# Recurrent branch projections as pairs of wide and narrow matmuls, with the opening and the attention heads reordered

## The chip, the core and the metric

The kernel runs on one core of one Trainium2 chip. The core has a matrix engine (TensorE, PE in the profile, with its weight loads as PEld), VectorE (DVE), ScalarE (ACT), GpSimd (POOL) and a queue engine (SyncE, SP) that issues transfers. The engines run their own instruction queues in order and wait for each other by semaphores. Matmuls write PSUM, a memory of eight banks; everything else lives in SBUF. The metric is the device time of one execution in microseconds; lower is better.

## The reference

Two residual layers on 256 tokens of 2048 features in float32. Layer 0 mixes tokens with attention (16 query heads, 4 key and value heads, RMS norm of queries and keys, axial rotary positions), layer 1 with a gated recurrence. Each is followed by a SwiGLU feed-forward layer of width 5632.

```python
def recurrent_mixer(h, w_in, conv_w, conv_b, w_a, b_a, w_i, b_i, lam, w_out):
    xy = h @ w_in
    xb, yb = jnp.split(xy, 2, axis=-1)
    yb = jax.nn.gelu(yb, approximate=True)
    xb = depthwise_conv_centred(xb, conv_w, conv_b)
    h_fwd = rg_lru(xb, w_a[0], b_a[0], w_i[0], b_i[0], lam[0], reverse=False)
    h_bwd = rg_lru(xb, w_a[1], b_a[1], w_i[1], b_i[1], lam[1], reverse=True)
    out = (h_fwd + h_bwd).astype(h.dtype) * yb
    return out @ w_out

def reference(x, ...):
    for i in range(DEPTH):
        h = rms_norm(x, norm_mix[i])
        mix = attention_mixer(...) if i % N_MIXERS == 0 else recurrent_mixer(...)
        x = x + mix
        x = x + swiglu(rms_norm(x, norm_ffn[i]), ffn_w_gate[i], ffn_w_up[i], ffn_w_down[i])
    return x
```

## The kernel before

Activations lie with features on the partitions and the 256 tokens along the row, in 16 tiles of 128 features. To keep float32 accuracy every operand is split in two parts that the matrix engine takes at its fast rate: hi (rounded) and lo (the rest). A product needs three of the four partial products: hi·hi, hi·lo and lo·hi.

**Weights.** `half()` (L124) takes the next block from a list `order` (L114 on): 8 tiles of 128 x 128, 512 KB. `load_half` (L84) issues its transfer into `raw` on SP, casts it to `hi` on ACT (L93), and writes the difference `lo` on DVE (L94). raw, hi and lo have five buffers each, so loads run ahead of PE by at most five blocks.

**Two forms of projection.** `project` (L168) uses `blocks` (L159): for each weight tile one matmul of 512 columns (the hi weights against the activation's hi and lo side by side) and one of 256 columns (the lo weights against hi) that adds into the right half of the PSUM bank, so that the result is the sum of the bank's two halves. `project_sum` (L179) uses `three` (L174): three matmuls of 256 columns into one half of the bank; nothing is left to be summed, and the other half is free as work space. Attention and feed-forward layers use pairs; the recurrent branch projections and the last down projection use threes.

**PE's order is written by hand.** `step()` (L145) is called after every weight tile and counts a clock; `later(d, f)` puts a piece of work (scores, transposes, gate matmuls) into PE's stream d steps on. The constants KEYS, VALUE, USUAL, LATE, WHEN and WHEN_LAST (L39 to L45) are such delays. The order on ACT, DVE, POOL and SP is planned by the framework from a model of costs.

**Opening.** The key projection runs first: eight blocks, each of 4 feature tiles for 2 of the 4 key heads (L363). The input x arrives in 256 KB or 512 KB pieces between them (`load_x`, L318), is scaled by the norm's gains on ACT (L252), and its lo part is made on DVE (L255). The 1/rms of the first norm is applied late; its squares are taken from a second copy of x in token order, four loads of 512 KB into `raw` buffers (`token_squares`, L332). Then come four value projections and 16 query heads (`attend`, L420): rotary on POOL (L374 to L376), split on DVE (L213, L214), squares (L437), scores (L442), softmax, scaling on POOL (L457), transposes (`turn`, L463), product with the values (L472).

**Output projections** (`output`, L188) of both mixers work through the first halves of four outputs, then through 6 of the 8 tiles of the second halves of two, and only then need the mixer's last two tiles.

**Recurrent stage** (L657 on): eight blocks of 256 channels. In each iteration PE runs two convolution branch projections of the next block, two gelu branch projections of this one, and between them this block's gate matmuls. `conv_branch` (L558) multiplies the projection by 1/rms (`nr.r`) from PSUM into an SBUF row with borders (L563), takes the first tap on ACT into the bank's free half (L565), three more on DVE (L568), and splits the result (L213, L214) for the gates. `gelu_branch` (L574) multiplies by 1/rms into the bank's free half, which holds the branch until the block is finished.

Of the kernel before, what the change touches and what calls it, by code (L numbers as in the profile page):

```python
# [18 lines left out]
P = 128  # L19
S = 256  # L20
# [36 lines left out]
AXES = [64 * a + 32 * h + f for h in range(2) for a in range(2) for f in range(32)]  # L57


@with_exitstack  # L60
def trunk(ctx, tc, w, out):
# [22 lines left out]
    def load_half(src, n, pieces=None):  # L84
# [3 lines left out]
        for a, b, then in pieces or ((0, n, None),):  # L88
            sl = slice(a, b)
            sync.dma_start(out=raw[:, sl, :], in_=src[:, sl, :])  # L90
            if then:
                then()
            act.copy(hi[:, sl, :], raw[:, sl, :])  # L93
            dve.tensor_tensor(lo[:, sl, :], raw[:, sl, :], hi[:, sl, :].bitcast(F32), ALU.subtract)  # L94
        return [(hi[:, i, :], lo[:, i, :]) for i in range(n)]
# [9 lines left out]
    def ffn_order(l):  # L105
# [3 lines left out]
        for p, n in enumerate(PARTS):  # L109
            more = units[at[p + 1] : at[p + 2]] if p + 1 < len(PARTS) else []  # L110
            seq += more[:1] + [halves(w[f"w_down{l}_{p}"][j], n) for j in range(KT)] + more[1:]
        return sum(seq, [])

    order = [(w["w_k"][i], HALF) for i in range(2 * KT // 4)]  # L114
# [9 lines left out]
    def half():  # L124
        n = taken[0]
        taken[0] += 1
        if n == 0:
            x2 = [partial(load_x, 2 * i, 2) for i in range(2)]
            return load_half(*order[n], ((0, 2, x2[0]), (2, 4, x2[1]), (4, HALF, None)))
        if n < KT // 2 and n % 2 == 0:  # L130
            load_x(2 * n, 4)
        if n == KT // 2 - 2:
            load_tables()
        if KT // 2 - 1 <= n < KT // 2 + 3:
            token_squares(n - KT // 2 + 1)
# [32 lines left out]
    def project(xs):  # L168
        acc = new_acc()
        for k0 in range(0, len(xs), HALF):  # L170
            blocks(acc, half(), xs, k0, len(xs))
# [7 lines left out]
    def project_sum(xs):  # L179
# [6 lines left out]
        return acc, bank[:, S:]  # L186

    def output(xs, ready, norm, close):  # L188
# [3 lines left out]
        late = [half() for j in range(2)]  # L192
# [4 lines left out]
        for j in range(KT):  # L197
            if j < 2:
# [5 lines left out]
        norm.finish_later()  # L204

    def evac(acc, tag):
        t = tmp(tag, bufs=3 if tag == "hy" else 2)
        act.copy(t, acc[:, S:])  # L208
# [3 lines left out]
    def split(dst, src):  # L212
        dve.tensor_copy(dst[:, :S], src)  # L213
        dve.tensor_tensor(dst[:, S:], src, dst[:, :S].bitcast(F32), ALU.subtract)  # L214

# [22 lines left out]
    class Norm:  # L238
# [9 lines left out]
        def scale(self, k, eng=act):  # L248
            g = col(self.g[0], self.g[1] + k)
            t = xp.tile([P, 2 * S], F32R, tag="xg", name=nm("xg"), bufs=16)  # L250
            if eng is act:
                act.activation(t[:, :S], x_sb[k], AF.Copy, scale=g)  # L252
            else:
                eng.tensor_scalar(t[:, :S], x_sb[k], g, 1.0, ALU.mult, ALU.mult)
            dve.scalar_tensor_tensor(t[:, S:], x_sb[k], g, t[:, :S].bitcast(F32), ALU.mult, ALU.subtract)  # L255
            self.xs.append(t)

# [9 lines left out]
        def finish_later(self):  # L267
            later(NORM, self.finish)
# [30 lines left out]
    def table_op(i):  # L299
        if prev[0] is not None:  # L300
            tc.add_manual_dep(
                i.ins, prev[0].ins.name,
                mybir.DependencyInfo(mybir.DependencyClass.NoSync, mybir.DependencyReason.DATA),
                reason="activation tables",
            )
# [12 lines left out]
    def load_x(k0, n):  # L318
        a = k0 % 4
        sync.dma_start(out=xq[k0 // 4][:, a : a + n, :], in_=w["x"][:, k0 : k0 + n, :])  # L320
        for k in range(k0, k0 + n):
            n0.scale(k)
# [9 lines left out]
    def token_squares(c):  # L332
        raw = wp.tile([P, HALF, P], F32, tag="raw", name=nm("raw"), bufs=5)
        sync.dma_start(out=raw, in_=w["xt"][c])
        act.activation(raw, raw, AF.Square, accum_out=msq[:, c // 2, c % 2 : c % 2 + 1])
# [11 lines left out]
    def first_rms():  # L347
# [3 lines left out]
        dg = tmp("hq")  # L351
# [3 lines left out]
        r_t.append(rsqrt(ms, "rt0"))  # L355
        pst = ps_m.tile([P, 2 * S], F32, tag="pm", name=nm("pm"))
# [6 lines left out]
    for i in range(2 * KT // 4):  # L363
        wt = half()
        for j in range(2):
            blocks(k_acc[2 * (i % 2) + j], wt[4 * j : 4 * j + 4], n0.xs, 4 * (i // 2))
# [11 lines left out]
    def key(h, acc):  # L378
        y = evac(acc, "hy")
        sq = tmp("hsq")  # L380
# [16 lines left out]
    kT = [ap.tile([P, 2 * S], F32R, tag=f"kT{h}", name=f"kT{h}", bufs=1) for h in range(NKV)]  # L397
    vt = [ap.tile([P, 2, 2, P], F32R, tag=f"vt{h}", name=f"vt{h}", bufs=1) for h in range(NKV)]
    for h in range(NKV):
        key(h, k_acc[h])  # L400
# [15 lines left out]
    for h in range(NKV):  # L416
        value(h, project(n0.xs))
    sync.dma_start(out=pk[:, PK0:], in_=w["pk"][:, PK0:])

    def attend(h, acc, dst):  # L420
        late = h >= NQ - 1
        eng = dve if late else pool
        d_sum, d_sc, d_turn, d_val = LATE[h - NQ] if h >= NQ - 2 else USUAL
# [5 lines left out]
        split(qs, q)  # L429
# [9 lines left out]
        def scores():  # L439
# [8 lines left out]
            dve.tensor_tensor(mx, mx, f, ALU.mult)  # L448
# [29 lines left out]

        later(d_sum, sums)
# [40 lines left out]
    def ffn(l, norm, nxt):  # L520
# [13 lines left out]
        for p, n in enumerate(PARTS):  # L534
            last = p == len(PARTS) - 1
            cur = hid
            hid = [] if last else [unit(bounds[p + 1])]
            for j in range(KT):
                if last and j == KT - 1:
                    dve.tensor_tensor(x_sb[j], x_sb[j], project_sum(cur)[0], ALU.add)  # L540
                    if nxt is not None:
                        nxt.add(j)
                else:
                    add_residual(j, project(cur), nxt if last else None)
# [12 lines left out]
    scope.append(rt.enter_context(tc.tile_pool(name="rp", bufs=2)))  # L557
    def conv_branch(ct):  # L558
        acc, run = project_sum(nr.xs)
# [3 lines left out]
        dve.tensor_tensor(b[:, 2 : S + 2], acc, nr.r, ALU.mult)  # L563
# [32 lines left out]
    class Block:  # L596
# [40 lines left out]
        def scan(self, d, j):  # L637
# [3 lines left out]
            h = tmp("h", bufs=4)  # L641
# [111 lines left out]
```

## Time and profile before

| | us |
|---|---|
| median of three runs | 2072.32 (2071.57 to 2072.38) |
| the profiled execution | 2072.61 |
| its span, first to last instruction | 2070.8 |
| mean granted TensorE clock | 0.999 |

The profiled execution is 1.8 us longer than its span, the time from the first to the last instruction. In the profile's lists, a line reads: source line, engine, operation, result and operands by name, shapes, count, then busy time and mean duration in ns, then the engine's idle time before the instructions and whom it waited for. A line can be that of a helper. In a timeline the columns are start, duration, engine, line, operation, with idle time and releaser in brackets. A matmul's shown duration contains its latency, so matmuls overlap; the distance between starts is the pace.

### The profile page before, as it was taken

The numbers are of one execution on the slowest core, as the hardware profiler recorded it, in microseconds if no ns is written. First come the engines' busy times: TensorE is split into PE (matmuls) and PEld (weight loads), VectorE is DVE, ScalarE is ACT, GpSimd is POOL, SyncE is SP. The second block draws the span as 40 slices with busy tenths as digits, with TensorE's granted clock in tenths as the row PEclk, the third lists the DMA queues.
The fourth block names the chain that finished last, engine by engine and source line by source line (L and its number), as shares of the span: only waits on it lengthen the run. The fifth ranks groups of instructions, "written<-read, shape, count | busy, mean of one in ns | idle before, by whom it ended". The sixth has DMA issues, their size and how long they took to land.

```text
span 2070.8 us, 32880 instructions
## 1 busy us (share of the span) xinstructions
PE 2060.8 (100%) x12528; PEld 1829.3 (88%) x12528; DVE 1448.1 (70%) x2152; ACT 1069.3 (52%) x1603; POOL 389.0 (19%) x394
## 2 busy tenths in 40 slices
PE   9999999999999999999999999999999999999999
PEld 7898888888888888888999998888888888888888
DVE  7889876665666666668878878766665666666665
ACT  7666444443344434444589995544443444444442
POOL 1463521110011000113334433311100111001100
PEclk9999999999999999999999999999999999999999
DMA  8544655555555565556655545555555555565564
GB/s 296 166 138 148 218 184 186 191 191 186 192 186 191 176 192 201 184 183 187 195 178 178 190 153 193 182 191 190 192 186 190 188 189 184 183 202 186 192 191 136
DMA packets 112766, 386.39 MB, mean 187 GB/s; under 512 B 12640, under 2 KB 15072, under 8 KB 112608
## 3 DMA queue, kind: packets, MB, share of 16 engines
q1 hardware_dynamic: 112464, 384.26, 56.5%
q8 instruction: 99, 1.62, 0.3%
q14 instruction: 59, 0.48, 0.1%
q10 hardware_dynamic: 144, 0.02, 0.0%
HBM read 382.13 MB, written 2.10 MB: 186 GB/s over the span
## 4 chain that ended last, share of the span: by engine, by line
PE 91%; POOL 4%; DVE 3%; issue 1%; ACT 1%; DMA 0%; SPq 0%; POOLq 0%; ACTq 0%; DVEq 0%
PE acc L165 80%; PE acc L175 3%; PE acc L176 3%; PE acc L177 3%; POOL hb L374 2%; DVE lo L94 1%; PE pm L176 1%; PE pm L177 1%; PE pm L175 1%; POOL pr L457 1%; POOL hq L375 1%; POOL hq L376 1%; ACT L309 0%; DMA raw<-in_w_k_dram 0%; ACT sg L309 0%
## 5 line engine op out<-in xcount | busy, mean ns | idle before, releaser
L94 DVE TENSOR_TENSOR lo<-raw,hi 128x1024 fp32r<-128x1024 f32 (+1 forms) x722 | 886.4, 1228 | 352.9 <-ACT hi L93 343.5
L93 ACT CAST hi<-raw 128x1024 fp32r<-128x1024 f32 (+1 forms) x722 | 741.7, 1028 | 594.6 <-PE acc L165 409.7
L165 PE MATMUL acc<-xg,hi 128*128 128x512 f32 x3200 | 1013.3, 396 | 1.8 <-DVE xg L255 1.7
L165 PEld LDWEIGHTS acc<-xg,lo 128*128 128x128 f32 x3200 | 601.4, 188 | 142.0 <-DVE lo L94 3.1
L165 PE MATMUL acc<-xg,lo 128*128 128x256 f32 x3200 | 638.4, 279 | 1.0 <-DVE lo L94 0.9
L165 PE MATMUL acc<-act,hi 128*128 128x512 f32 x1892 | 596.5, 396 | 0.1
L165 PEld LDWEIGHTS acc<-xg,hi 128*128 128x128 f32 x3200 | 490.7, 189 | 2.9 <-DVE xg L255 2.2
L165 PEld LDWEIGHTS acc<-act,lo 128*128 128x128 f32 x1892 | 355.4, 188 | 84.8 <-DVE act L213 1.3
L165 PE MATMUL acc<-act,lo 128*128 128x256 f32 x1892 | 372.9, 278 | 1.0 <-DVE act L213 1.0
L525 POOL TENSOR_TENSOR fg<-fg,nr 128x256 f32<-128x256 f32 x88 | 118.7, 1349 | 1187.3 <-ACT fg L309 1187.3
L165 PEld LDWEIGHTS acc<-act,hi 128*128 128x128 f32 x1892 | 288.9, 189 | 0.3 <-DVE act L214 0.3
L175 PE MATMUL acc<-xg,hi 128*128 128x256 f32 x512 | 144.8, 283 | 0.0
L176 PE MATMUL acc<-xg,hi 128*128 128x256 f32 x512 | 144.6, 282 | 0.0
L177 PE MATMUL acc<-xg,lo 128*128 128x256 f32 x512 | 144.4, 282 | 0.0
L208 ACT COPY fg<-acc 128x256 f32<-128x256 f32 x88 | 33.0, 375 | 152.9 <-PE acc L165 152.9
L208 ACT COPY fu<-acc 128x256 f32<-128x256 f32 x88 | 32.9, 374 | 148.2 <-PE acc L165 148.2
L177 PEld LDWEIGHTS acc<-xg,lo 128*128 128x128 f32 x512 | 97.9, 191 | 0.0
L175 PEld LDWEIGHTS acc<-xg,hi 128*128 128x128 f32 x512 | 97.9, 191 | 0.0
L176 PEld LDWEIGHTS acc<-xg,hi 128*128 128x128 f32 x512 | 97.9, 191 | 0.0
L209 DVE TENSOR_TENSOR fg<-acc,fg 128x256 f32<-128x256 f32 x88 | 37.4, 425 | 79.7 <-ACT fg L208 79.6
L209 DVE TENSOR_TENSOR fu<-acc,fu 128x256 f32<-128x256 f32 x88 | 37.4, 425 | 74.3 <-ACT fu L208 74.3
L291 DVE TENSOR_TENSOR x<-x,acc 128x256 f32<-128x256 f32 x126 | 52.9, 420 | 41.8 <-PE acc L165 41.8
(171 smaller groups left out, 1435.5 us busy)
## 6 DMA issues: line engine op xcount, KB each, us to landing
raw<-in_w_gate_dram SPq DMA_DIRECT2D x176, 512.0 KB, 3.6
raw<-in_w_up_dram SPq DMA_DIRECT2D x176, 512.0 KB, 3.6
raw<-in_w_down_dram SPq DMA_DIRECT2D x128, 512.0 KB, 3.6
raw<-in_w_in_dram SPq DMA_DIRECT2D x64, 512.0 KB, 3.9
raw<-in_w_down_dram SPq DMA_DIRECT2D x64, 384.0 KB, 3.1
raw<-in_w_qv_dram SPq DMA_DIRECT2D x40, 512.0 KB, 3.8
raw<-in_w_o_dram SPq DMA_DIRECT2D x32, 512.0 KB, 3.7
raw<-in_w_out_dram SPq DMA_DIRECT2D x32, 512.0 KB, 3.7
```

The costliest lines, as they stand in the source:

```text
L93: act.copy(hi[:, sl, :], raw[:, sl, :])
L94: dve.tensor_tensor(lo[:, sl, :], raw[:, sl, :], hi[:, sl, :].bitcast(F32), ALU.subtract)
L165: pe.matmul(o, w, x, start=(k == 0 and not part), stop=(k == total - 1 and not part))
L175: pe.matmul(o, hi, x[:, :S], start=start, stop=False)
L176: pe.matmul(o, hi, x[:, S:], start=False, stop=False)
L177: pe.matmul(o, lo, x[:, :S], start=False, stop=stop)
L208: act.copy(t, acc[:, S:])
L209: dve.tensor_tensor(t, acc[:, :S], t, ALU.add)
L291: dve.tensor_tensor(x_sb[j], x_sb[j], acc[:, :S], ALU.add)
L374: eng.tensor_tensor(b[64 * j : 64 * j + 64], y[64 * i : 64 * i + 64], s[64 * i : 64 * i + 64], ALU.mult)
L375: eng.tensor_tensor(dst, y, c, ALU.mult)
L525: pool.tensor_tensor(g, g, norm.r, ALU.mult)
```

## The change

- **Recurrent branches.** Both branches call `project` (pairs). `halves_sum` adds the bank's halves in one VectorE reduction over a view that puts the two halves innermost; GpSimd then multiplies by 1/rms in place. The gelu branch lands in an SBUF tile with four buffers instead of staying in PSUM. The backward scan writes over a gate tile that is no longer needed, and `h` has two buffers instead of four.
- **Opening.** The key weights are laid out anew (`KEY_TILES`): six blocks of 2 feature tiles for all 4 heads, then two of 4 tiles for 2 heads. x comes first, the scaling of each pair of tiles is ordered behind a cast by `follow`, an edge that only sets the order on an engine. The first weight block is one transfer cast in four pieces instead of three transfers. The token copy of x is one load of 2 MB into a tile of its own, which keys and values use later. The first value projection's weights are loaded and cast ahead of the keys' evacuation. FIRST and KEYS are 5 to 8 steps later; the squares of keys 2 and 3 have buffers of their own.
- **Heads.** A query's split waits OPERAND = 8 steps and is ordered behind the previous head's softmax maximum. The first head and the last three have delays of their own.
- **Output and feed-forward.** `output` holds three second halves instead of two (HELD), and the norm behind it comes 2 steps later. The last down projections of each layer begin with two outputs side by side.

```diff
+HELD = 3
-FIRST = 17
+FIRST = 22
-KEYS = (24, 26, 30, 33)
+KEYS = (29, 31, 35, 41)
+FIRST_HEAD = (17, 22, 16, 10)
 USUAL = (17, 22, 15, 7)
-LATE = ((10, 23, 15, 13), (5, 15, 17, 9))
+LATE = ((17, 22, 15, 12), (10, 23, 15, 13), (7, 16, 16, 9))
+OPERAND = 8
...
+KEY_TILES = [[(2 * i + k, j) for j in range(NKV) for k in range(2)] for i in range(KT // 2 - 2)]
+KEY_TILES += [[(KT - 4 + k, j + h) for h in range(2) for k in range(4)] for j in (0, 2)]
...
+    def load_half(src, n, pieces=1, then=None):
...
+        newest["load"] = sync.dma_start(out=raw[:, :n, :], in_=src[:, :n, :])
+        if then:
+            then()
+        for i in range(pieces):
+            sl = slice(i * n // pieces, (i + 1) * n // pieces)
+            newest["cast"] = act.copy(hi[:, sl, :], raw[:, sl, :])
             dve.tensor_tensor(lo[:, sl, :], raw[:, sl, :], hi[:, sl, :].bitcast(F32), ALU.subtract)
...
         if n == 0:
+            load_x(0, 2)
+            scale_x(0)
+            return load_half(*order[n], 4, partial(load_x, 2, 2))
+        if n == 1:
+            scale_x(1)
+            return load_half(*order[n], 2)
...
-        late = [half() for j in range(2)]
+        late = [half() for j in range(HELD)]
...
-        norm.finish_later()
+        norm.finish_later(NORM + 2)
...
+    first_value = [half() for _ in range(2)]
+    follow(sync.dma_start(out=x_tok, in_=w["xt"]), newest["load"])
     for h in range(NKV):
+        if h == 2:
+            token_squares(0)
         key(h, k_acc[h])
...
-        split(qs, q)
+        def operand():
+            i = split(qs, q)
+            if "mx" in newest:
+                follow(i, newest["mx"])
...
+            begun = []
+            if last:
+                begun = [new_acc() for _ in range(2)]
+                for k0 in (0, HALF):
+                    for acc in begun:
+                        blocks(acc, half(), cur, k0, n)
...
+    def halves_sum(dst, acc):
+        dve.tensor_reduce(dst, acc.rearrange("p (h s) -> p s h", h=2), AX.X, ALU.add)
+
     def conv_branch(ct):
-        acc, run = project_sum(nr.xs)
+        acc = project(nr.xs)
+        run = acc[:, S:]
...
-        dve.tensor_tensor(b[:, 2 : S + 2], acc, nr.r, ALU.mult)
+        halves_sum(b[:, 2 : S + 2], acc)
+        pool.tensor_tensor(b[:, 2 : S + 2], b[:, 2 : S + 2], nr.r, ALU.mult)
...
     def gelu_branch(ct):
-        acc, y = project_sum(nr.xs)
-        if ct >= KT - 2:
-            y = tmp("gl")
-        dve.tensor_tensor(y, acc, nr.r, ALU.mult)
+        acc = project(nr.xs)
+        y = tmp("gl", bufs=4)
+        halves_sum(y, acc)
+        pool.tensor_tensor(y, y, nr.r, ALU.mult)
         return y
...
-            h = tmp("h", bufs=4)
+            h = self.gate[3, j] if d else tmp("h")
```

More of the change, by code (lines that the diff above doesn't have):

```diff
@@ L329, in trunk, with token_squares @@
     r_t = []
[L332 to L335, printed above, removed]
+    x_tok = ap.tile([P, 2, D], F32, tag="kv", name="x_tok", bufs=1)
+    def token_squares(a):
+        for i in range(2):
+            t = x_tok[:, a, i * D // 2 : (i + 1) * D // 2]
+            newest["cast"] = follow(act.activation(t, t, AF.Square, accum_out=msq[:, a, i : i + 1]), newest["cast"])
     def load_tables():
@@ L477, in scores @@
             later(d_turn, turn)
+        later(OPERAND, operand)
         later(d_sum, sums)
```

113 lines of the change are left out of this document (64 added, 49 removed).

## The prediction

> **What bounds the kernel now.** I read the page's first part, then busy time by stretch, then TensorE's waits, then its timeline at each wait.
>
> ```profile
> PE 2060.8 (100%) x12528; PEld 1829.3 (88%) x12528; DVE 1448.1 (70%) x2152; ACT 1069.3 (52%) x1603; POOL 389.0 (19%) x394
> ...
> PE 91%; POOL 4%; DVE 3%; issue 1%; ACT 1%; DMA 0%; SPq 0%; POOLq 0%; ACTq 0%; DVEq 0%
> ...
> L177 PE MATMUL acc<-xg,lo 128*128 128x256 f32 x512 | 144.4, 282 | 0.0
> ```
>
> TensorE (PE) is busy throughout and carries 91% of the chain that ended last. So time can only come from matmuls that stream faster, or from the few places where PE stands still. The two forms of projection can be compared in the stretches where PE never waits:
>
> ```profile
> 300.00:900.00 600.00, 600.00 (x3447) 523.50 (x3446) 381.15 (x516) 264.79 (x337) 53.09 (x39) 1.00 0.57 189
> ...
> 1040.00:1200.00 160.00, 160.00 (x1341) 160.00 (x1341) 134.57 (x220) 144.02 (x244) 59.89 (x79) 1.00 0.56 183
> ```
>
> Columns: length, then busy time and count of PE, weight loads, DVE, ACT, POOL, then granted clock, DMA share, GB/s. In the first feed-forward stage (pairs) a matmul takes 600/3447 = 0.1741 us, so a tile of two takes 0.348. In the recurrent stage (threes) it is 160/1341 = 0.1193, so a tile of three takes 0.358. The waits of PE in the whole run (us in total, times, longest):
>
> ```profile
> PE acc L165 <- DVE xg L255: 1.7, 2, 1.4
> ...
> PE acc L165 <- DVE act L213: 1.0, 1, 1.0
> PE acc L165 <- DVE lo L94: 0.9, 1, 0.9
> PE pm L176 <- DVE pT L467: 0.7, 1, 0.7
> PE pm L388 <- ACT hsq L381: 0.6, 1, 0.6
> PE pm L274 <- POOL ss L265: 0.4, 2, 0.2
> PE pm L463 <- POOL pr L457: 0.3, 1, 0.3
> ```
>
> Few and short: whatever the change does to waits can bring some 5 us, plus what the opening gives.
>
> **Pairs instead of threes.** The L177 row counts 512 tiles (32 projections of 16). Each goes from 0.358 to 0.348: 512 x 0.0098 = 5.0 us less. It has no cover to lose, since PE sets the end here; the bounds are 0 (if PE is held elsewhere) and 5.5.
>
> What it adds per projection: the sum of halves reads 512 elements where L563 read 256, and GpSimd does the multiply.
>
> ```profile
> L563 DVE TENSOR_TENSOR cb<-acc,nr 128x256 f32<-128x256 f32 x16 | 6.7, 416 | 1.0 <-PE acc L177 0.9
> L447 DVE TENSOR_REDUCE mx<-pm 128x2 f32<-128x512 f32 x16 | 10.8, 678 | 0.0
> L375 POOL TENSOR_TENSOR hq<-hy,rope 128x256 f32<-128x256 f32 x15 | 11.1, 740 | 1.2
> L525 POOL TENSOR_TENSOR fg<-fg,nr 128x256 f32<-128x256 f32 x88 | 118.7, 1349 | 1187.3 <-ACT fg L309 1187.3
> L213 DVE CAST act<-fu 128x256 fp32r<-128x256 f32 x88 | 25.4, 288 | 0.0
> L213 DVE CAST xs<-xc 128x256 fp32r<-128x256 f32 x16 | 13.5, 847 | 0.3
> ```
>
> The nearest row for the sum is L447, also a reduction of 512 PSUM elements: 0.68, so 0.26 more on DVE. It makes 2 results where the new one makes 256; the trace cannot show whether that costs. The multiply takes 0.74 to 1.35 on POOL. The same cast takes 0.29 in the feed-forward and 0.85 here, where POOL runs beside it: a multiply can cost DVE from nothing to its whole length, 1.35; I take 0.3, about half of the cast's 0.56. A block of 80 tiles lasts 28.6 us, in which DVE works 134.57/160 of the time, 24.1, and ACT 144.02/160, 25.8. The new block lasts 64 x 0.348 + 16 x 0.358 = 28.0; DVE gets 4 x 0.56 = 2.2 more, 26.3 or 94%; ACT is at 92%. Both still fit, so inside the blocks I take 0. That PE's row of this stage shows no idle time says the loads run ahead today.
>
> The Trainium skill, "SBUF — State Buffer", section "Who interferes with whom", goes further: VectorE and GpSimd share one port pair under an exclusive lock, and whoever comes second is fully blocked; its list has tensor_reduce as never contending. By that the sum of halves itself is safe, and the casts and differences beside the multiplies pay; the cast's 0.85 agrees with it. Its full form is the slower rival below.
>
> One place has no slack: the first gates come 18 steps after the first convolutions.
>
> ```profile
> 1023.89 0.42 DVE L563 TENSOR_TENSOR cb<-acc,nr 128x256 f32<-128x256 f32 x1
> ...
> 1028.25 0.43 DVE L214 TENSOR_TENSOR xs<-xc,xs 128x256 fp32r<-128x256 f32 x1
> ...
> 1028.98 0.28 PE L175 MATMUL pm<-xs,ghi 128*128 128x256 f32 x1
> ```
>
> Their second operand is done at 1028.68 and read at 1028.98: 0.3 us to spare. The new chain is longer by 0.26 + 0.74 (to 1.35), and PE arrives 32 x 0.0098 = 0.3 earlier. So PE waits 1.0 to 1.6 less whatever the queue gives back; I take **+1.0**, bounds 0 and +2.5 (another cast of 1 us ahead of it). Later blocks have 50 steps, 17 us, and hide it.
>
> **The opening.**
>
> ```profile
> 5.39 0.50 PE L165 MATMUL acc<-xg,hi 128*128 128x512 f32 x1 [0.26 <-DVE xg L255]
> ...
> 7.76 0.72 PE L165 MATMUL acc<-xg,hi 128*128 128x512 f32 x1 [1.40 <-DVE xg L255]
> ...
> 10.01 1.04 ACT L93 CAST hi<-raw 128x1024 fp32r<-128x1024 f32 x1 [0.64 <-DMA raw<-in_w_k_dram]
> ...
> 13.10 1.99 ACT L93 CAST hi<-raw 128x1024 fp32r<-128x1024 f32 x2
> ...
> 15.45 0.50 PE L165 MATMUL acc<-xg,lo 128*128 128x256 f32 x2
> ```
>
> ```profile
> 9.00:10.00 1.00, 0.91 (x2) 0.29 (x1) 0.60 (x1) 0.36 (x1) 0.00 (x0) 0.50 1.00 352
> ...
> 16.00:18.00 2.00, 2.00 (x13) 1.75 (x12) 2.00 (x5) 2.00 (x5) 0.00 (x0) 1.00 1.03 407
> ```
>
> 64 key pairs need 22.3 us but last from 5.39 to 32.04 (31.81, below, plus one wide matmul), 4.4 too many, all before 15.45. PE waits for the input's scaled tiles, then runs at half clock, and the DMA share is 1.00: bytes decide. Before pair 16 both versions must have 2.5 MB (five blocks of 512 KB), so they land no earlier but for the larger pieces. What is won is order: the third load waits for 2 scalings (0.9 us of ACT) and not 4. I expect pair 16 about 1 us earlier and 0.3 from fewer pieces: **-1.3**. Bounds: -2.8 (half clock and waits gone, first matmul 1 us later) and +0.5 (one whole 512 KB load ahead of the first matmul instead of 128 KB).
>
> The four token loads (2 MB) become one behind the first value loads on SP; at 407 GB/s it takes 5.2 us. Behind it stands the second value projection's load, needed 16 pairs (5.6 us) after the keys end, near 36. Even if the token load were issued as late as 25 it would be in by 31, so it is hidden; without that cover its lateness would count in full.
>
> **The waits by place** (start to start, less 0.12 for a narrow or 0.23 for a wide matmul):
>
> ```profile
> 31.81 0.63 PE L165 MATMUL acc<-xg,hi 128*128 128x512 f32 x2
> 33.38 0.51 PE L165 MATMUL acc<-xg,lo 128*128 128x256 f32 x2 [0.94 <-DVE lo L94]
> ...
> 46.61 0.28 PE L165 MATMUL acc<-xg,lo 128*128 128x256 f32 x1
> 47.45 0.70 PE L388 MATMUL pm<-hsq,ones 128*128 128x256 f32 x2 [0.56 <-ACT hsq L381]
> ...
> 79.27 0.28 PE L165 MATMUL acc<-xg,lo 128*128 128x256 f32 x1
> ...
> 79.80 1.00 PE L463 MATMUL pm<-cn,pr 128*128 128x128 f32 x4 [0.25 <-POOL pr L457]
> ...
> 183.97 0.35 PE L175 MATMUL pm<-pT,vt 128*128 128x256 f32 x1
> 185.06 0.39 PE L176 MATMUL pm<-pT,vt 128*128 128x256 f32 x1 [0.74 <-DVE pT L467]
> ...
> 276.45 0.28 PE L165 MATMUL acc<-xg,lo 128*128 128x256 f32 x1
> 276.93 0.71 PE L274 MATMUL pm<-ss,ones 128*128 128x128 f32 x4 [0.21 <-POOL ss L265]
> ...
> 1255.54 0.28 PE L165 MATMUL acc<-act,lo 128*128 128x256 f32 x1
> 1256.78 0.38 PE L165 MATMUL acc<-act,lo 128*128 128x256 f32 x1 [0.96 <-DVE act L213]
> ```
>
> - 31.81: the first value projection's lo, queued behind key work on DVE. Its casts now come ahead of that: **-1.1** (0 if DVE takes it late again).
> - 46.61: the last key's squares shared two buffers; now four, and the stage is 8 steps later: **-0.7** (to 0).
> - 79.27: turn one step (0.35) later: **-0.4** (to -0.7).
> - 183.97: the values come 5 steps (1.7 us) later, the wait was 0.97: **-0.9** (to 0).
> - 276.45 and its twin (two waits at L274): 2 steps, 0.7, against 0.36 each: **-0.7** (to 0).
> - 1255.54: 1.1 lost on the last mixer tile. A third held load gives 6 pairs more cover, 2.1 us; PE arrives 0.3 earlier and DVE has 0.5 more to do: 1.3 left against 1.1, **-1.1** (to 0). Behind PE there stand only its own matmuls.
>
> The delayed split, the buffers of h and gl, and the two interleaved last projections cost nothing: PE shows no wait at those places, and what covers them is PE's own stream; without it each would cost its 0.4 to 0.8 of DVE.
>
> **Sum**: -5.0 + 1.0 - 1.3 - 1.1 - 0.7 - 0.4 - 0.9 - 0.7 - 1.1 = -10.2. The profiled execution took 2072.6 (span 2070.8 and 1.8 around it), 0.3 above the median of the runs. 2072.3 - 10.2 = **2062**.
>
> **Rivals.** (a) *DVE becomes the bound* of the recurrent stage, slower. It decides once a projection adds more than (28.0 - 24.1)/4 = 0.97 us to DVE. With 0.26 and a full lock for 1.35 it is 1.61: a block takes 24.1 + 6.4 = 30.5, 2.5 too many, 20 over eight blocks, less what the loads run ahead (five buffers of 8 tiles, 14 us at most; I take 5): 2062 + 15 = 2077. For it: 0.85 against 0.29. Against: POOL already works 59.89 of 160 us here, and PE does not wait; DVE works on PSUM much of the time. (b) *New waits replace the old*: +2.5 at the first gates, opening +0.5, half of the 4.9 of waits back: -5.0 + 2.5 + 0.5 - 2.5 = -4.5, so 2068. For it: the order on DVE and ACT is planned anew. (c) *Everything lands*: -5.5 - 2.8 - 5.5 = -13.8, 2058.5. Against: the opening is at full DMA share.
>
> **Chances.** Forecast 0.45, (a) 0.20, (b) 0.20, (c) 0.15. Within 0.2% (4.1 us; less than that is not told from no change) falls half of (b): 0.10; faster 0.70; slower 0.20. The range leaves out (a): 2057 to 2070; the forecast's own is 2059.5 to 2065.
>
> **What would show it.** The recurrent stage's matmuls at 0.174 us with no wait of L165 there; the sum near 0.68 and the multiply between 0.74 and 1.35; DVE below 95% in the blocks; one wait of about 1 us at the first gates; pair 16 near 14.3 and the values' first matmul near 31; no wait at L388, L274 or on the last act tile. Wrong if PE waits for lo tiles inside the blocks, or if the sum takes well over 0.7.

## The result and the profile after

The changed kernel takes 2075.58 us (median of 20 runs), the kernel before 2072.35: a ratio of 1.0014, 95% interval 1.0007 to 1.0020. It is slower by 3.2 us: the interval leaves out 1, but the loss is less than the 0.2% that the prediction itself counts as no change. Forecast were 2062 and a range of 2057 to 2070. The profiled execution took 2076.15, its span 2074.4.

The page's first part and the chain that ended last:

```profile
PE 2057.7 (99%) x12016; PEld 1803.7 (87%) x12016; DVE 1470.8 (71%) x2154; ACT 1068.5 (52%) x1605; POOL 424.1 (20%) x426
...
PE 86%; DVE 7%; ACT 3%; issue 2%; POOL 1%; DMA 1%; SPq 0%; ACTq 0%; POOLq 0%; DVEq 0%
PE acc L197 83%; DVE lo L113 3%; ACT L341 1%; DMA graw<-in_w_gates_dram 1%; ACT sg L341 1%; POOL glo L657 1%; ACT hi L112 1%; DVE act L248 0%; DVE sg L709 0%; PE pm L209 0%; PE pm L208 0%; PE pm L207 0%; DMA raw<-in_w_k_dram 0%; DVE acc L633 0%; POOL cb L628 0%
```

512 matmuls fewer, as forecast. But TensorE's share of the chain fell from 91% to 86%: VectorE, ScalarE and the gate loads now stand in it. TensorE's waits (us in total, times, longest):

```profile
PE pm L207 <- DVE h L707: 5.3, 1, 5.3
PE acc L197 <- DVE lo L113: 3.3, 4, 1.0
PE pm L207 <- DVE xs L247: 1.5, 1, 1.5
...
PE pm L208 <- DVE pT L520: 0.7, 1, 0.7
PE pm L208 <- DVE xs L248: 0.5, 1, 0.5
PE acc L197 <- ACT hi L112: 0.5, 2, 0.3
PE pm L516 <- POOL pr L510: 0.4, 1, 0.4
```

The waits at L388 (keys), L274 (norms) and on the last mixer tile are gone. In their place stand the first gates (xs), weight tiles inside the blocks (lo, hi) and one wait of 5.3 us (h). By stretches, each from the first narrow matmul of one stage to that of the next in the two traces (the last to the last matmul):

| stretch | before | after | change | forecast |
|---|---|---|---|---|
| span's start to the first query head | 59.51 | 54.59 | -4.92 | -3.1 |
| query heads | 118.75 | 119.49 | +0.74 | -0.4 |
| first output projection | 95.40 | 94.69 | -0.72 | -0.9 |
| first feed-forward layer | 736.77 | 736.29 | -0.47 | -0.35 |
| recurrent stage | 229.76 | 240.75 | +10.99 | -4.0 |
| second output projection | 90.79 | 89.17 | -1.61 | -1.1 |
| second feed-forward layer | 736.40 | 735.92 | -0.48 | -0.35 |

So the change gained 7.5 us elsewhere and lost 11.0 in the stage it is named after: 1.63 in the iteration of the first gates and the one ahead of it, 1.35 in the six after them, 8.01 in the last. Busy times and counts there (columns as in the prediction):

```profile
1040.00:1200.00 160.00, 156.88 (x970) 139.09 (x969) 143.00 (x211) 140.17 (x238) 79.52 (x94) 1.00 0.52 172
...
1050.00:1190.00 140.00, 137.86 (x861) 122.84 (x860) 128.03 (x189) 120.35 (x206) 72.23 (x84) 1.00 0.54 179
...
1231.96:1238.79 6.83, 5.11 (x20) 4.73 (x21) 5.12 (x10) 6.05 (x10) 1.45 (x2) 0.50 0.25 87
```

TensorE stands idle for 3.1 of 160 us, and VectorE is busy 128.03/140 = 91%. How a block loses time, from the timelines of the engines:

```profile
1023.24 1.22 DVE L113 TENSOR_TENSOR lo<-raw,hi 128x1024 fp32r<-128x1024 f32 x1
1024.38 0.29 DVE L247 CAST xs<-xc 128x256 fp32r<-128x256 f32 x1
1024.58 0.68 DVE L619 TENSOR_REDUCE cb<-acc 128x256 f32<-128x512 f32 x1
1024.72 0.39 PE L207 MATMUL pm<-xs,ghi 128*128 128x256 f32 x1 [1.47 <-DVE xs L247]
1025.18 0.42 DVE L248 TENSOR_TENSOR xs<-xc,xs 128x256 fp32r<-128x256 f32 x1
...
1156.70 1.55 POOL L628 TENSOR_TENSOR cb<-cb,nr 128x256 f32<-128x256 f32 x1 [0.97 <-DVE cb L619]
1158.29 0.57 ACT L630 ACTIVATE acc<-cb,pk 128x256 f32<-128x256 f32 x1 [1.87 <-POOL cb L628]
...
1163.06 1.04 ACT L112 CAST hi<-raw 128x1024 fp32r<-128x1024 f32 x1
1164.13 1.49 DVE L113 TENSOR_TENSOR lo<-raw,hi 128x1024 fp32r<-128x1024 f32 x1 [0.98 <-ACT hi L112]
1165.68 0.50 PE L197 MATMUL acc<-xg,lo 128*128 128x256 f32 x2 [1.02 <-DVE lo L113]
...
1233.68 0.58 PE L207 MATMUL pm<-xs,ghi 128*128 128x256 f32 x1 [5.31 <-DVE h L707]
```

The second group is one block: ScalarE stands 1.87 us at the first tap for GpSimd's product, everything queued behind it is late, its weight cast (hi) among it, then VectorE's difference (lo), then TensorE. The last row is the last block's third gate: it needs a PSUM bank that the block before frees with a late scan (L707). The granted clock is 0.50 from 1231.96, 1.7 us before this wait ends, to 1238.79.

A measure that shows the loss before TensorE waits is the **lead** of a weight block: the time from the end of its lo difference to the first matmul that reads it. In the rows above it is 1165.68 - 1165.62 = 0.06 us. The smallest lead in each of six successive blocks (the third block on): before 5.43, 5.40, 5.39, 5.39, 5.10, 5.39; after 4.48, 2.81, 0.05, 0.06, 0.05, 0.05. The engines behind the loads fell back by up to 2.8 us a block until the lead was used up; from there a block lasts 29.6 us instead of 28.06. So TensorE's pace shows how slow these engines are only after the lead is gone.

### The profile page after: what moved, and what is told of

Same layout as the page of the kernel before. It is cut to its first block, busy times and chain, and to the rows that moved or that the text cites. A ratio compares the mean times of both kernels' runs of the same rounds, so it can differ in the third digit from the quotient of the medians.

```text
span 2074.4 us, 31834 instructions
## 1 busy us (share of the span) xinstructions
PE 2057.7 (99%) x12016; PEld 1803.7 (87%) x12016; DVE 1470.8 (71%) x2154; ACT 1068.5 (52%) x1605; POOL 424.1 (20%) x426
## 4 chain that ended last, share of the span: by engine, by line
PE 86%; DVE 7%; ACT 3%; issue 2%; POOL 1%; DMA 1%; SPq 0%; ACTq 0%; POOLq 0%; DVEq 0%
PE acc L197 83%; DVE lo L113 3%; ACT L341 1%; DMA graw<-in_w_gates_dram 1%; ACT sg L341 1%; POOL glo L657 1%; ACT hi L112 1%; DVE act L248 0%; DVE sg L709 0%; PE pm L209 0%; PE pm L208 0%; PE pm L207 0%; DMA raw<-in_w_k_dram 0%; DVE acc L633 0%; POOL cb L628 0%
## 5 line engine op out<-in xcount | busy, mean ns | idle before, releaser
L197 PE MATMUL acc<-xg,hi 128*128 128x512 f32 x3712 | 1176.0, 396 | 0.6 <-ACT hi L112 0.5
L197 PE MATMUL acc<-xg,lo 128*128 128x256 f32 x3712 | 743.5, 279 | 3.4 <-DVE lo L113 3.3
L197 PEld LDWEIGHTS acc<-xg,hi 128*128 128x128 f32 x3712 | 570.0, 189 | 1.9 <-ACT hi L112 1.8
L327 DVE TENSOR_TENSOR x<-x,acc 128x256 f32<-128x256 f32 x126 | 52.9, 419 | 41.6 <-PE acc L197 41.6
L301 POOL TENSOR_TENSOR ss<-ss,sq 128x256 f32<-128x256 f32 x45 | 61.6, 1370 | 3.5
L299 POOL TENSOR_TENSOR sq<-x 128x256 f32<-128x256 f32 x45 | 41.0, 910 | 104.1 <-DVE x L328 100.4
L657 POOL TENSOR_TENSOR glo<-graw,ghi 128x512 fp32r<-128x512 f32 x32 | 54.2, 1695 | 8.1 <-ACT ghi L656 7.8
L328 DVE TENSOR_TENSOR x<-x,acc 128x256 f32<-128x256 f32 x126 | 53.0, 420 | 4.0
L290 DVE SCALAR_TENSOR_TENSOR xg<-x,pk,xg 128x256 fp32r<-128x256 f32 x64 | 50.2, 796 | 0.4 <-ACT xg L287 0.4
```

What stands on the lines that cost most here:

```text
L197: pe.matmul(o, w, x, start=(k == 0 and not part), stop=(k == total - 1 and not part))
L301: pool.tensor_tensor(self.ss, self.ss, sq, ALU.add)
L327: dve.tensor_tensor(x_sb[j], x_sb[j], acc[:, :S], ALU.add)
L328: dve.tensor_tensor(x_sb[j], x_sb[j], acc[:, S:], ALU.add)
L657: pool.tensor_tensor(lo, raw, hi[:].bitcast(F32), ALU.subtract)
```

## The experiments

Each ratio is to the kernel before, with its 95% interval. A run "loses lead" by so many us a block, read as above. VectorE's, ScalarE's and GpSimd's orders are planned anew in every build, so differences under about 1 us in stages that an edit doesn't touch are not read.

**1, 2. Which part loses.** The old branches in the changed kernel, and the new branches alone in the kernel before.

```diff
-        acc = project(nr.xs)
+        acc, run = project_sum(nr.xs)
...
-        halves_sum(b[:, 2 : S + 2], acc)
-        pool.tensor_tensor(b[:, 2 : S + 2], b[:, 2 : S + 2], nr.r, ALU.mult)
+        dve.tensor_tensor(b[:, 2 : S + 2], acc, nr.r, ALU.mult)
...
```

> The changed kernel with the recurrent branches as before: threes, the product with 1/rms in one VectorE operation, the gelu input in PSUM, four h buffers. My theory (the loss is in the recurrent stage): the opening, heads and output gains stay (stage starts 5.4 us earlier at the recurrent stage, 1.6 more on the last mixer tile), so 2065 us (2063 to 2067), and TensorE does not wait for lo inside the blocks. Rival (the loss comes from the new order of weight loads and buffers around it): 2070 or more.

> The kernel before with only the recurrent branches changed. My theory: the whole loss and more, 2082 us (2079 to 2085): the 10 us that the recurrent stage lost between its first matmul and the output projection. Rival (the stage loses only because the shorter opening and heads leave it later or earlier loads): 2067, the 5 us of the pairs.

2065.26 us (0.9964, 0.9951 to 0.9976), leads at 5.1 to 5.4, no wait on a weight tile; and 2080.37 (1.0041, 1.0028 to 1.0053). Both as the theory had it: the recurrent edit costs 8 us alone and 10 with the rest of the change, and the rest is worth 7 alone and 5 with it.

**3, 4. GpSimd's product.** On VectorE instead, and left out.

```diff
-        pool.tensor_tensor(b[:, 2 : S + 2], b[:, 2 : S + 2], nr.r, ALU.mult)
+        dve.tensor_tensor(b[:, 2 : S + 2], b[:, 2 : S + 2], nr.r, ALU.mult)
...
-        pool.tensor_tensor(y, y, nr.r, ALU.mult)
+        dve.tensor_tensor(y, y, nr.r, ALU.mult)
```

> The changed kernel with the product with 1/rms moved from GpSimd to VectorE, as a second operation after the sum of halves. Theory T1 (the product's latency in GpSimd's queue stalls ScalarE at the first tap, and so the next weight cast): ScalarE's wait at the first tap falls from 18 us to about 5, a block lasts 28.1 instead of 29.6, 2066 us. Theory T2 (VectorE's load decides): four products of 0.4 us a block more on VectorE, a block lasts 30 or more, 2080 us or more.

> The changed kernel without the product with 1/rms in the recurrent branches (that part of the computation is left out). T1 and T2 both expect a gain, and it bounds what the product costs: T1 (its latency and its place in GpSimd's queue are all of the loss inside the blocks) a block of 28.1 us and 2064 us. If the longer sum or the gelu input in SBUF bear the loss, a block stays above 29 us and the time above 2071.

With the product on VectorE 2075.62 (1.0015, 1.0006 to 1.0024): neither time. Busy times in its blocks, then in those of the run without the product:

```profile
1050.00:1190.00 140.00, 138.56 (x865) 123.54 (x864) 138.55 (x209) 121.98 (x208) 62.92 (x65) 1.00 0.54 180
```

```profile
1050.00:1190.00 140.00, 140.00 (x881) 125.90 (x880) 125.85 (x195) 127.28 (x215) 57.73 (x70) 1.00 0.54 180
```

With the product on VectorE, VectorE works 99% of the time and is the bound by itself. From one weight difference to the same one in the next block it takes 29.0 to 30.1 us, on average 29.6. So T2 had the mechanism and nearly the block; its 2080 us left out that the first blocks live on the lead, in which TensorE still runs at 28.06. Without the product 2068.10 (0.9977, 0.9968 to 0.9986): TensorE does not wait in the blocks, yet the lead goes 5.09, 4.02, 3.17, 2.32, 1.26, 0.71, and the last block's gate still waits 4.0 us. So the product is not all of it. Here VectorE takes 28.6 to 29.1 us from one weight difference to the same one in the next block, and neither it nor ScalarE waits for TensorE for more than 0.3 of the 140 us.

**5. The memset in GpSimd's queue.** One pair of padded buffers, cleared once.

```diff
-        b = tmp("cb", (P, S + 4))
-        pool.memset(b[:, 0:2], 0.0)
-        pool.memset(b[:, S + 2 : S + 4], 0.0)
+        b = padded[ct % 2]
```

> The changed kernel with two fixed buffers for the convolution input, whose borders are cleared once, so that no memset stands in GpSimd's queue inside the blocks. Theory Q (GpSimd's in-order queue: the memset waits 17 us for VectorE's last tap, and the gate weights queued behind it come late, so ScalarE and the next weight cast do): GpSimd waits at the memset and ScalarE's waits for gate loads go, a block lasts 28.1 to 28.6 instead of 29.6, 2071 us (2069 to 2073). Rival V (VectorE's own load, 91.5%, makes the ring): no change, 2075 to 2077.

2078.53 (1.0032, 1.0020 to 1.0044): no gain, but 3 us more than the changed kernel. The theory of the memset falls; GpSimd only waits elsewhere (46 us at the product instead of 30).

**6. The last block's gates later.**

```diff
-WHEN_LAST = (5, 9, 13, 17, 19, 20, 21, 24, 24, 25, 26, 27, 33, 39, 39)
+WHEN_LAST = (18, 20, 22, 24, 25, 26, 27, 28, 28, 29, 30, 31, 35, 39, 39)
```

> The changed kernel with the last block's gates at steps 18, 20, 22, 24 instead of 5, 9, 13, 17, and its later work as near behind them as before at the end. Theory L (the 5.3 us wait of the last block's third gate and the half clock behind it are avoidable idle time, since TensorE has other matmuls to do meanwhile): both go, 2069 us (2067 to 2071). Rival: the last mixer tiles become late by as much, so the wait turns up in the output projection, 2074 or more.

2075.00 (1.0012, 1.0003 to 1.0021). The wait falls from 5.3 to 2.3 us, and the last iteration from 25.2 to 22.9. That hardly pays: half clock still follows (3.4 us instead of 6.8), and in the profiled execution it comes at the first gates too. A missed forecast: the work before the wait is late, not the place of the wait wrong.

**7, 8. Pairs in one branch alone.** The edit is the convolution half of run 1 for pairs in the gelu branch only, and this for pairs in the convolution branch only:

```diff
-        acc = project(nr.xs)
-        y = tmp("gl", bufs=4)
-        halves_sum(y, acc)
-        pool.tensor_tensor(y, y, nr.r, ALU.mult)
+        acc, y = project_sum(nr.xs)
+        if ct >= KT - 2:
+            y = tmp("gl")
+        dve.tensor_tensor(y, acc, nr.r, ALU.mult)
```

> The changed kernel with pairs and GpSimd's product in the gelu branch alone; the convolution branch as before (threes, product on VectorE). Theory Q: the product's latency hurts only where the first tap waits for it, so blocks last 28.3 and nearly the whole loss goes, 2063 us (2061 to 2066). Rival V (each branch costs VectorE the same): half of the loss stays, 2069 or more.

> The changed kernel with pairs and GpSimd's product in the convolution branch alone; the gelu branch as before (threes, product on VectorE into PSUM). Theory Q: the whole loss is here, 2074 us or more. Rival V: half of it, 2069 to 2071. If the gelu input in SBUF is what costs (finish operations of 1.0 us instead of 0.41), 2064 to 2067.

2066.10 (0.9970, 0.9959 to 0.9982) and 2066.90 (0.9972, 0.9962 to 0.9982). The gelu branch alone costs 0.8 us against run 1, the convolution branch alone 1.6, both together 10: a threshold, not a sum. With pairs in the gelu branch the lead falls by 0.5 us a block (5.17 to 2.57) and the last block's gate waits 2.2. With pairs in the convolution branch it stays at 5.36, though ScalarE waits 14.3 us in the whole stage at the tap (18.2 in the changed kernel); only the first gates lose (2.0 us, and half clock behind them).

**9 to 11. Doses of work.** The changed kernel without the decay's square; and on run 1's kernel one more square on ScalarE, or one more step on VectorE.

```diff
-            q = tmp("sq", bufs=4)
-            act.activation(q, a, AF.Square)
+            q = a
```

```diff
             act.activation(q, a, AF.Square)
+            act.activation(q, a, AF.Square)
```

```diff
+            dve.scalar_tensor_tensor(tmp("rsq_t"), q, 1.0, th, ALU.add, ALU.mult)
             dve.scalar_tensor_tensor(th, q, 1.0, th, ALU.add, ALU.mult)
```

> The changed kernel without the square in the decays (that part of the computation is left out): four ScalarE operations of 0.41 us a block less, 1.66 us, nothing else taken from any engine. Theory S (ScalarE's in-order queue is the ring: its 25.4 us of work a block plus 3.9 us of its waits for VectorE, GpSimd and loads exceed TensorE's 28.06): a block falls from 29.6 to 28.06, the late weight casts go, 2068 us (2064 to 2071). Rival V (VectorE's load decides): blocks stay near 29.6, 2075 us.

> The kernel with the recurrent branches as before and the rest as changed (2065.3 us), with the square in the decays done twice: 1.66 us more ScalarE work a block. Theory S: ScalarE had 0.9 us a block of waits for TensorE to spare, so the smallest lead of a weight load falls by some 0.7 us a block from 5.4, and the last block's gates come late: 2066 to 2071. Rival V: no change of the leads, 2065.

> The same kernel (branches as before, 2065.3 us), with the step of the decays on VectorE done twice: 4 x 0.41 = 1.66 us more VectorE work a block, none on ScalarE. Theory S: the leads stay near 5.4 us, or fall only by what the scans make ScalarE wait, 2065 to 2066. Rival V: the leads fall, 2067 or more.

2068.37 (0.9981, 0.9972 to 0.9990): the time that theory S gave, but not by its mechanism. The lead still falls by some 1.0 us a block to 0.05, with VectorE now the full queue (132.72 of 140 us busy, and 5.7 waiting for the tap). 2071.40 (0.9994, 0.9985 to 1.0002): lead lost, 0.4 a block instead of 0.7 (5.44 to 3.38), and 3.2 us of waiting at the last block's gate. 2071.51 (0.9992, 0.9983 to 1.0001): lead nearly kept (5.43 to 4.22), but time was lost, in the profiled execution, the fastest of them (2068.39), at the last block's gate (2.8 us, behind the scan). So neither queue alone is the bound; each has little to spare, and the last block pays for what the queues are behind.

**12. The first block.** Pairs in the convolution branches of blocks 1 to 7 only.

```diff
+        if ct < 2:
+            acc, run = project_sum(nr.xs)
+        else:
+            acc = project(nr.xs)
+            run = acc[:, S:]
...
```

> Pairs and GpSimd's product only in the convolution branches of blocks 1 to 7; the first block's convolutions and all gelu branches as before. If the 2 us at the first gates come from the longer chain of the first block alone, and one branch of pairs fits in ScalarE's ring: 14 x 16 x 0.0098 = 2.2 us below 2065.3, so 2063 us. Otherwise 2065 to 2067.

2064.07 (0.9960, 0.9948 to 0.9973); no wait of TensorE in the stage. The wait at the first gates is the first block's longer chain. The time is 1.2 us below run 1, of 2.2 expected; the recurrent stage itself is 1.7 shorter.

**13, 14. The heads,** on run 12's kernel: the split at once; then the delays as before too.

```diff
-        later(OPERAND, operand)
+        operand()
...
-LATE = ((17, 22, 15, 12), (10, 23, 15, 13), (7, 16, 16, 9))
+LATE = ((10, 23, 15, 13), (5, 15, 17, 9))
```

> The kernel with conv pairs after the first block (2064.1 us), with each head's split made at once instead of 8 steps later behind the previous head's maximum. Its head stage lasts 119.7 us, against 118.8 in the kernel before. If the delayed split is what put the new waits there (at the transposed probabilities): the head stage 119.0 or less, 2063.3 us. If the other delays did: no change of the stage, 2064. If the split at once blocks VectorE ahead of the maxima: longer, 2065.

> The same, with the delays of the first and the last heads also as before. My prediction's reasons (the wait at the first turn, 0.4, and at head 13's values, 0.9, come back): the head stage 1.3 us longer than in the run with the split at once. If they were worth nothing on the whole: the stage as before, 118.8, 2063.1 us.

2063.39 (0.9954, 0.9941 to 0.9966) and 2063.77 (0.9955, 0.9943 to 0.9968). The head stage lasts 119.3, then 118.9; the output projection behind it 94.3, then 95.3. The split at once is worth less than the scatter between builds (119.3 to 119.7 where the heads are as changed, 119.8 with the split at once in run 18). The old delays give the heads 0.4 and take 1.0 from the projection: part of what the new ones save at head 13 they lose before it.

**15. The order of the key tiles,** on run 12's kernel.

```diff
-KEY_TILES = [[(2 * i + k, j) for j in range(NKV) for k in range(2)] for i in range(KT // 2 - 2)]
...
+KEY_TILES = [[(4 * (i // 2) + k, 2 * (i % 2) + j) for j in range(2) for k in range(4)] for i in range(KT // 2)]
...
```

> The same kernel (2064.1 us), with the key tiles in the order of before (each load four input tiles by two heads, not two by four), and the input scaled for it; all else of the new opening kept. The opening's key stage gained 3.8 us where I had predicted 1.3. If the order of the tiles is the reason (the second load needs no further input tiles), the value projections start 2.5 us later, at 32.2, and 2066.6 us. If the single larger load and the later token squares are: 29.7 and 2064.

2064.37 (0.9959, 0.9946 to 0.9971): the value projections start 0.57 us later, not 2.5. Of the 3.8 us that the expectation names 1.1 is the first value's wait; of the remaining 2.7 the order is the smaller part. By that the rest lies in the loads and casts that this run kept (below).

**16 to 18. Where the gelu branch lives.** On run 12's kernel, pairs in the gelu branches with the product on VectorE into PSUM; the same edit alone in the changed kernel; and on run 12's kernel together with the split at once. In runs 16 and 18 `t` has the default number of buffers instead of four.

```diff
-        y = tmp("gl", bufs=4)
-        halves_sum(y, acc)
-        pool.tensor_tensor(y, y, nr.r, ALU.mult)
+        t = tmp("gl", bufs=4)
+        halves_sum(t, acc)
+        y = t if ct >= KT - 2 else acc[:, S:]
+        dve.tensor_tensor(y, t, nr.r, ALU.mult)
```

> The same kernel (2064.1 us), with pairs in the gelu branches too, their product with 1/rms on VectorE and written to PSUM, so that neither GpSimd's queue nor SBUF operands beside it are used. TensorE needs 2.5 us less in all. Theory S (ScalarE's queue is full at 28.4 us a block with one branch of pairs): a block of 28.06 is not kept, the smallest lead falls by 0.3 to 0.8 us a block and the last block's gates come late: 2063.5 to 2067. Rival (only GpSimd's product and the SBUF operands hurt): leads stay, 2061.5 us.

> The changed kernel with one edit: the gelu branch's product with 1/rms on VectorE and written to PSUM (in the last block to SBUF), instead of on GpSimd and in SBUF. Pairs in both branches, GpSimd's product before the first tap, the first block's convolutions and the heads stay as changed. Theory G (the gelu input in SBUF, where VectorE's finish works beside GpSimd, and its product in GpSimd's queue tip the balance): no late weight loads, lead falling by 0.3 us a block, and only the 2.4 us at the first gates left of the loss: 2064.9 us (2064 to 2067). Theory S (ScalarE's wait for GpSimd's product at the first tap, 1.9 us a block, is enough): late loads as in the changed kernel, 2071 or more.

> Pairs in both branches with the gelu product on VectorE into PSUM, threes in the first block's convolutions, and each head's split at once. If the two gains add up (0.4 for the split, 1.6 for the gelu pairs): 2062.0 us (2061.5 to 2062.8), faster than every kernel so far.

2062.48 (0.9948, 0.9935 to 0.9962), 2066.32 (0.9970, 0.9959 to 0.9982) and 2062.85 (0.9954, 0.9941 to 0.9968). The first and the last are the fastest kernels here and are not told apart; the two gains didn't add up. Run 16 lies between its two theories: the lead falls by 0.3 us a block (5.07 to 3.78), but the last block's gate waits only 0.3. The middle one tells most: that one edit takes 9.3 us off the changed kernel. Its leads are 5.08, 5.08, 5.08, 4.78, 4.63, 4.97, a block lasts 28.06 with pairs in both branches, and the last block's wait is gone. Its blocks, then VectorE's groups in them:

```profile
1050.00:1190.00 140.00, 140.00 (x880) 125.86 (x879) 128.32 (x211) 129.01 (x220) 67.01 (x80) 1.00 0.57 188
```

```profile
L248 DVE TENSOR_TENSOR xs<-xc,xs 128x256 fp32r<-128x256 f32 x10 | 6.3, 626 | 0.2
L643 DVE TENSOR_TENSOR acc<-gl,nr 128x256 f32<-128x256 f32 x10 | 6.1, 615 | 0.2
...
L248 DVE TENSOR_TENSOR act<-acc,act 128x256 fp32r<-128x256 f32 x10 | 4.2, 418 | 0.0
```

The same groups of the changed kernel, its cast for the gates and its longer sums:

```profile
L248 DVE TENSOR_TENSOR xs<-xc,xs 128x256 fp32r<-128x256 f32 x9 | 12.7, 1416 | 0.3
L247 DVE CAST xs<-xc 128x256 fp32r<-128x256 f32 x9 | 4.1, 452 | 0.1
L248 DVE TENSOR_TENSOR act<-gl,act 128x256 fp32r<-128x256 f32 x10 | 9.6, 964 | 0.0
L619 DVE TENSOR_REDUCE cb<-acc 128x256 f32<-128x512 f32 x10 | 6.8, 678 | 0.0
L619 DVE TENSOR_REDUCE gl<-acc 128x256 f32<-128x512 f32 x9 | 6.1, 677 | 0.0
```

With the edit VectorE does two products more a block, and yet has 25.7 us of work a block (128.32 in 140, at 28.06) instead of 27.1 (128.03 in 140, at 29.6): the mixer tile's difference falls from 0.96 to 0.42 us when its source lies in PSUM, the gates' from 1.42 to 0.63. The gates' difference reads SBUF in both kernels, so with it only the order and what GpSimd does beside it have changed. ScalarE's waits in this stretch, in the changed kernel and then with the edit:

```profile
ACT acc L630 <- POOL cb L628: 8.4, 5, 1.9
ACT pm L341 <- DVE h L707: 4.6, 5, 1.0
ACT pm L341 <- DVE sg L709: 2.9, 5, 0.6
ACT ghi L656 <- DMA graw<-in_w_gates_dram: 2.4, 2, 1.5
```

```profile
ACT pm L341 <- DVE h L708: 4.0, 5, 1.0
ACT ghi L657 <- PE pm L208: 1.5, 2, 0.8
...
ACT pm L341 <- DVE sg L710: 1.0, 5, 0.2
```

In the changed kernel ScalarE's 120.35 us of work and these 18.3 of waiting all but fill the 140 us, and none of the waits is for TensorE: ScalarE is behind. With the edit it waits for TensorE again. The convolution's product is still on GpSimd, but no longer late for the tap.

**What is settled and what is open.** Every run with the gelu branch in SBUF and pairs in both branches loses lead (the changed kernel and runs 2 to 6 and 9), even without any product of GpSimd (run 4), and so does run 7 with pairs in that branch alone. Every run with it in PSUM and no work added keeps it, or loses on average at most 0.3 a block, with GpSimd's product before the tap or without. Run 4 is the closest comparison: it has no products at all, and yet its VectorE has more work a block than run 17's (26.0 us, 125.85 in 140 at 28.9, against 25.7) and its lead falls by 1.0 a block. So it is the gelu branch in SBUF, with the orders that the framework plans for it, that tips the balance. Not separated are VectorE's longer operations and the order planned around them. Nor was the gelu product tried on VectorE with its result left in SBUF and the rest as changed: what run 17 gains by taking this product from GpSimd is not told apart from what it gains by PSUM.

## Why the prediction was wrong

- **Step that failed: "Both still fit, so inside the blocks I take 0."** The prediction's own sign of being wrong, TensorE waiting for lo tiles inside the blocks, came true. The loads themselves were sized well. Before, VectorE's work showed in this row:

```profile
1050.00:1190.00 140.00, 140.00 (x1175) 140.00 (x1174) 119.87 (x196) 126.96 (x215) 54.25 (x70) 1.00 0.57 188
```

  VectorE had 24.5 us of work a block (119.87 us in 140, at 28.67 a block) and got 27.1 (128.03 in 140, at 29.6), 0.63 more a projection against the forecast 0.56, and below the 0.97 at which rival (a) was to decide. What was wrong is the criterion that work below TensorE's time fits. A share under 95% was taken to mean that the stage keeps TensorE's pace. But VectorE, ScalarE and GpSimd wait for each other in order, and waits belong to the loop: ScalarE had 86% of work and 13% of waits. The lead of 5.4 us hid it for three blocks. Rival (a)'s 2077 is near the measured time by luck: VectorE by itself becomes the bound only in run 3.
- **The price of GpSimd beside VectorE** was put at 0.3 a multiply, on VectorE's casts, and "the buffers of h and gl ... cost nothing". The sum came out by luck, for the parts were others. The same groups before:

```profile
L213 DVE CAST xs<-xc 128x256 fp32r<-128x256 f32 x10 | 10.1, 1006 | 0.2
L214 DVE TENSOR_TENSOR xs<-xc,xs 128x256 fp32r<-128x256 f32 x10 | 6.4, 637 | 0.3
L214 DVE TENSOR_TENSOR act<-acc,act 128x256 fp32r<-128x256 f32 x10 | 4.1, 411 | 0.0
```

  The gates' cast became shorter (1.01 to 0.45 us) and the differences longer: the gates' from 0.64 to 1.42, the mixer tile's from 0.41 to 0.96. Moving the gelu branch to SBUF gave the mixer tile's difference two SBUF operands. The Trainium skill, "SBUF — State Buffer", section "Who interferes with whom", says that a VectorE instruction with at most one SBUF input, outside its two-port modes, does not contend with GpSimd, and that one with two SBUF inputs contends with a GpSimd instruction that reads SBUF. The trace agrees, with 0.96 us from SBUF against 0.42 from PSUM; and in run 3, where GpSimd has no product, the same difference from SBUF takes 0.42 (though 0.69 in run 4, which has none either). The prediction drew on that section for the reduction and overlooked this.
- **The last block** was not in the sum: +8.0 us, 5.3 of waiting and the rest mostly half clock. It comes with the engines that are behind: one edit removes both (run 17). A small lead is not needed for it, for in run 11 the lead was 4.2 or more and the gate still waited 2.8.
- **Pairs, -5.0**: right where TensorE doesn't wait. From the third block's start to the last iteration's, run 17's edit makes six blocks 3.6 us shorter than before, 0.61 each, as 64 x 0.0098 = 0.63 has it.
- **First gates, +1.0, bounds 0 and +2.5**: 2.0 us of waits, near the upper bound and by the mishap named there: the rows at 1023.24 show a lo difference ahead of the split, and the next sum between its two operations. The slack was read a little short: the row at 1028.98 reads the cast, done at 1028.22, and the difference is read at 1029.10, so 0.4 us were to spare and not 0.3.
- **Opening, first value and keys, -1.3 - 1.1 - 0.7**: -4.9. The value projections start 3.8 us earlier: 1.1 is their own wait, gone as forecast, and 2.7 the opening's, forecast 1.3 with a bound of 2.8. The value stretch gained 1.1 where 0.7 were expected. The opening's size was wrong because the step took the bytes to move as decisive and their rate as fixed. Before, and after:

```profile
4.00:6.00 2.00, 1.74 (x12) 1.50 (x11) 1.52 (x4) 1.21 (x3) 0.00 (x0) 1.00 0.79 231
6.00:8.00 2.00, 0.60 (x4) 0.28 (x3) 0.85 (x3) 0.91 (x2) 0.00 (x0) 0.97 1.01 319
8.00:10.00 2.00, 1.91 (x5) 1.02 (x4) 0.70 (x2) 0.62 (x1) 0.00 (x0) 0.50 1.00 348
```

```profile
4.00:6.00 2.00, 1.71 (x9) 1.41 (x8) 1.14 (x4) 1.45 (x4) 0.00 (x0) 1.00 1.04 377
6.00:8.00 2.00, 2.00 (x10) 1.64 (x11) 2.00 (x6) 1.71 (x6) 0.00 (x0) 1.00 0.98 379
8.00:10.00 2.00, 2.00 (x13) 1.69 (x12) 1.59 (x4) 1.89 (x4) 0.00 (x0) 1.00 0.99 397
```

  The last three numbers of a row are granted clock, DMA share and GB/s. In these 6 us the fewer, larger transfers bring 2.3 MB where the pieces brought 1.8. Run 15, with the tile order of before but the larger transfers, brings 2.2. That the size of the pieces is the reason is read from these rows; it wasn't tried by itself. The half clock of before (7.87 to 11.29) was not the loss: run 2, with the opening of before, shows none there and starts its query heads at the same 59.51.
- **Heads and head 13, -0.4 - 0.9**: the output projection gained 0.7 of the 0.9 forecast, the heads lost 0.74; together nothing. The stretches with the norm waits and the last mixer tile gained somewhat more than forecast (0.5 each against 0.35, and 1.6 against 1.1).

With the gelu branch in PSUM and the first block in threes the change does bring the time that was forecast, 2062. In part that is luck: in run 16 the opening gives 1.3 us more than forecast, and the heads 1.3 less.

## What to carry to other kernels

Before you let an engine's share rise towards 90%, add its waits on the other in-order engines to its work, and watch the lead of the loads block by block: it shows a loop that is too slow long before the bound engine stands still. A result that moves from PSUM to SBUF can make its readers slower where GpSimd works beside them (here one reader took 0.96 us instead of 0.41), so price the readers, not only the operation that moves. Test parts one by one and in pairs: here two edits that cost 0.8 and 1.6 us cost 10 together.

## What the runs showed of the hardware

- The reduction that adds two PSUM halves (512 elements to 256 results) takes 0.68 us, the same as one to 2 results, and stays at that in every run, whatever GpSimd does beside it.
- Around a stall of TensorE the granted clock stood at 0.50 for about 3.4 us (7.9 to 11.3 before, after a wait of 1.4; 1025.6 to 1029.1 in run 17, after 1.45 and 0.55) or for twice as long (6.8 us with waits of 4.0 in run 4 and of 5.0 to 5.3 in the changed kernel and runs 2, 3 and 5). The length of the wait alone doesn't decide whether it comes: waits of 1.4 to 1.5 and 0.5 to 0.6 at the first gates were followed by it in runs 2, 3, 6, 8 and 17, and not in the changed kernel and runs 5 and 9. In the last block waits of 2.2, 2.5 and 2.8 had none (runs 7, 9 and 11), one of 2.3 had 3.4 us (run 6).
